# Building the operands of the last eight pairs a second time instead of storing and reloading them, and splitting the output weights every fourth product

## The chip, the cores and the metric

The kernel runs on one core of one Trainium2 chip. The metric is the device time of one execution in microseconds (us), as a median of several runs.

## The reference

One decoder block for a sequence of 2048 tokens with 1024 channels, all in float32:

```
h      = rms_norm(x, g_norm) * (1 + scale) + shift      # shift, scale, gate from silu(c) @ w_mod
proj   = h @ w_in                                       # (2048 x 1024) @ (1024 x 8192)
x_rnn, z_rnn, q, k, v, z_attn, g_r, g_a = split(proj)   # eight parts of 1024 columns
y_rnn  = (rg_lru(conv(x_rnn)) * silu(z_rnn)) @ w_out_rnn
y_attn = (dilated_attention(rope(q), rope(k), v) * silu(z_attn)) @ w_out_attn
merged = sigmoid(g_r + bg_r) * y_rnn + sigmoid(g_a + bg_a) * y_attn
out    = rms_norm(x + gate * (merged @ w_o), g_final)
```

The change is in how the weights of the large product `h @ w_in` (all parts but v) and of `w_out_rnn` and `w_out_attn` are prepared for the tensor engine.

## The kernel before

**Precision.** A float32 number is used as a high part and a low part. `split_s` (line 208) makes both of a weight block: ScalarE copies it to the rounded type (`hi_act`, line 158), and GpSimd (POOL) subtracts that copy from the block (`lo_pool`, line 164). `mm3` (line 152) then does three matmuls: high by high, high by low, low by high.

**Pairs and products.** The 7168 columns of `w_in` other than v are taken 256 at a time, in 28 pairs of 128-column blocks. `pair_order` (line 1143) gives their order: eight recurrent pairs `("r", m)`, with gate pairs and "plain" query and key pairs between them, and then the last six, two rotated pairs (the 32 columns of each head that get rotary angles) with two plain ones behind each. The last six run in a stage of their own with its own buffers, and pairs 20 and 21 are the last two of the stage before it. A pair is multiplied by Strassen's scheme in seven products instead of eight (`strassen`, line 349), each of four `mm3` of 128x512, twelve matmuls. Their left operands are the blocks a11, a21, a22, a12 or sums of them; the right ones (B11, T2, T3, T1, B21, T4, B22) come from h. The products add up in PSUM tiles X, Z, W, V and Y. ScalarE copies X out after the first product (`u1`, line 385), VectorE adds Z and W to it (`u2`, `u3`), and the fifth product is added into X again, so it must wait for `u1`. The last product of a pair (into V) is held until after the first of the next pair.

**Two halves.** The tokens are done in two halves, `f` = 0 and 1 (1024 tokens each), each with the values stage (`values_half`) and then 28 x 7 = 196 products. In the first half each left operand is made from raw weights, by `operand_events` (line 263): for pair `x` it yields steps with a due time in products, counted from four products (`LEAD`) ahead of the pair's first. Raw loads of a11, a21, a22 and a12 (SyncE's queue, SP, line 253) come at -6, -5, -4 and -1, two sums and a split at 0, and so on to the last split at 6; three sums beside them run on VectorE (lines 284, 285, 293 and 298 in all). Two splits later, ScalarE's queue stores the finished operand (512 KB, high and low) to `sD` in HBM (lines 276 and 279). In the second half `load_next` (line 313) loads all 196 operands back from `sD` through SP, seven ahead.

Operands live in a ring of seven tiles `S0` to `S6`, raw blocks in a ring of five, `R0` to `R4`. `pump` runs due steps after each product; `late` and `after_prod` hold other steps by product number. The order of instructions on each engine is written out by hand (`manual_schedule`), so each engine's queue is in the order in which these steps are emitted.

**Other work at these places.** `output_weights` (line 422) splits the 32 half blocks of `w_out_rnn` and `w_out_attn` during the second half: load (a raw tile), a raw copy to `wR` for the second matrix, split into the tiles `s1` and `s2`, and store to `wD`, one block every five products. The sums of `operand_events` use tiles `s1` and `s2` too. At the end of the first half `next_norm` and `next_even` load x for the next half (line 512), square its rows on ScalarE (line 1242) and build right operands from it; at the end of the second, `residual_gate` sums w_mod columns on VectorE. When `load_next` is past the operands it loads the first output weights (`load_wd`) for the next stage, attention; the last four operands bring with them a load of `yaT` each (`load_yd`, line 346), four blocks that are split (`yh`, `yl`) before the first matmul of that stage.

Of the kernel before, what the change touches and what calls it, by code (L numbers as in the profile page):

```python
# [20 lines left out]
P = 128  # L21
# [6 lines left out]
KH = KT // 2  # L28
# [5 lines left out]

FILL = (2.85, 2.75)
MORE = 0.8
NEG = 1e30

TABLES = 24
# [14 lines left out]
def constants():  # L54
# [10 lines left out]
    old, prev, diag = q4, (d <= 0) + q4, np.where(d >= 0, 1 + q4, 0)  # L65
    add = np.array([NEG, 0.0, -math.log(2.0)])
    cst[:, K_M23 : K_M23 + 512] = add[np.concatenate([old, old, prev, diag], axis=1)]
# [22 lines left out]
def decoder_block(ctx, tc, x, c, positions, g_norm, w_mod, b_mod, w_in, b_gate, conv_w, conv_b,  # L90
# [10 lines left out]
    def scratch(name, shape):  # L101
        return nc.dram_tensor(name, shape, F32, kind="Internal").ap()
# [8 lines left out]
    yaT = scratch("yaT", [D, S])  # L111
# [4 lines left out]

    tabD = scratch("tabD", [2, 2, P, HALF])

    sD = scratch("sD", [28 * 7, P, 2, KH, P])

    wD = scratch("wD", [2, KT, 2, P, 2, KH, P])
    wR = scratch("wR", [KT, 2, P, KH, P])
# [34 lines left out]
    def hi_act(o, i):  # L157
        nc.scalar.activation(o, i, AF.Copy)  # L158
# [4 lines left out]
    def lo_pool(o, i, h):  # L163
        nc.gpsimd.tensor_tensor(o, i, h.bitcast(F32), ALU.subtract)  # L164
# [26 lines left out]
    def s_tile(shape):  # L191
        i = ring["S"] % NS
        ring["S"] += 1
        return T(pS if i < 4 else wS, shape, F32R, f"S{i}")
# [13 lines left out]
    def split_s(src):  # L208
        t = s_tile([P, 2, KH, P])
        hi_act(t[:, 0], src)  # L210
        lo_pool(t[:, 1], src, t[:, 0])
        return t
# [3 lines left out]
    n_prod, late, after_prod = [0], {}, {}  # L216
# [18 lines left out]
    kept = []  # L235
# [25 lines left out]
    LEAD = 4  # L261

    def operand_events(x, pieces):

        load, v = block_loads(pieces), {}
        tt = nc.vector.tensor_tensor

        def raw(name, i, half):
            v[name] = load(i, half)

        def split(i, name):
            first[7 * x + i] = t = split_s(v[name])
            kept.append((7 * x + i, t))
            if len(kept) > 2:
                k, t2 = kept.pop(0)
                nc.scalar.dma_start(sD[k], t2[:].bitcast(F32))
            while 7 * x + i == 28 * 7 - 1 and kept:
                k, t2 = kept.pop(0)
                nc.scalar.dma_start(sD[k], t2[:].bitcast(F32))

        def sums():
            for name in ("s1", "s2"):
                v[name] = T(wq, [P, KH, P], F32, name, bufs=1)[:]
            tt(v["s1"], v["a21"], v["a22"], ALU.add)
            tt(v["s2"], v["s1"], v["a11"], ALU.subtract)  # L285

        yield -6, lambda: raw("a11", 0, 0)
        yield -5, lambda: raw("a21", 1, 0)
        yield -4, lambda: raw("a22", 1, 1)
        yield -1, lambda: raw("a12", 0, 1)  # L290
        yield 0, sums
        yield 0, lambda: split(0, "a11")
        yield 1, lambda: tt(v["a21"], v["a11"], v["a21"], ALU.subtract)
        yield 1, lambda: split(1, "s2")
        yield 2, lambda: split(2, "a21")
        yield 3, lambda: split(3, "s1")
        yield 4, lambda: split(4, "a12")
        yield 5, lambda: tt(v["s2"], v["a12"], v["s2"], ALU.subtract)
        yield 5, lambda: split(5, "a22")
        yield 6, lambda: split(6, "s2")  # L300

    first, events = {}, []
# [10 lines left out]
    def load_next():  # L313
        n = n_loaded[0]
        n_loaded[0] += 1
        if n < 28 * 7:
            t = s_tile([P, 2, KH, P])
            nc.sync.dma_start(t[:].bitcast(F32), sD[n])
            loaded.append((n, t))
            if n >= 28 * 7 - KH:  # L320
                load_yd(yaT, 0, n - 28 * 7 + KH)
        else:
            k = n - 28 * 7
            if k < 3:
                load_wd(0, 0, k) if k < 2 else load_wd(0, 1, 0)
            if k == 1:

                t = T(hp, [P, KH, CH], F32, "T", bufs=14)
                nc.sync.dma_start(t[:], yaT[KH * P :, :CH].rearrange("(k p) j -> p k j", p=P))
                for i in range(KH):  # L330
                    Y0[True, 0, KH + i] = t[:, i, :]
# [10 lines left out]
    def load_yd(ys, n, k):  # L342
        x = n_y[0]
        n_y[0] += 1
        t = T(pR, [P, CH], F32, f"R{x % 4}")
        nc.sync.dma_start(t[:], ys[k * P : (k + 1) * P, n * CH : (n + 1) * CH])
        Y0[ys is yaT, n, k] = t

    def strassen(f, key, done):

        up = pu[0]
        x = pair_id[key]
        if f and x == 0:
            for _ in range(NS):
                load_next()
        n_op = iter(range(7 * x, 7 * x + 7))

        def take():
            if f:
                return (f, *loaded.pop(0))  # L360
            i = next(n_op)
            return f, i, first.pop(i)

        def prod(ps, b, first, last, op=None):
            f, i, s = op or take()
            bh, bl = B[b]
            for k in range(KH):
                mm3(ps[:], s[:, 0, k, :], s[:, 1, k, :], bh[:, k, :], bl[:, k, :],
                    first=first and k == 0, last=last and k == KH - 1, skip_group_check=True)
            n_prod[0] += 1  # L370
            if f:
                used.add(i)
                while n_loaded[0] - NS in used:
                    load_next()
            run_late(n_prod[0])

        X = T(pj, [P, CH], F32, "X", bufs=2)
        prod(X, "B11", True, False)
        last_product()
        Z = T(pj, [P, CH], F32, "Z")  # L380
        prod(Z, "T2", True, True)
        u1 = T(up, [P, CH], F32, "u1", bufs=1)
        u2 = T(up, [P, CH], F32, "u2", bufs=2)
        with tc.high_priority():
            nc.scalar.activation(u1[:], X[:], AF.Copy)  # L385
            nc.vector.tensor_tensor(u2[:], Z[:], u1[:], ALU.add)
        W = T(pj, [P, CH], F32, "W")
        prod(W, "T3", True, True)
        u3 = T(up, [P, CH], F32, "u3", bufs=1)
        with tc.high_priority():  # L390
            nc.vector.tensor_tensor(u3[:], W[:], u2[:], ALU.add)
        V = T(pj, [P, CH], F32, "V")
        prod(V, "T1", True, False)
        done(1, 1, V, u3)
        prod(X, "B21", False, True)
        done(0, 0, X, None)
        Y = T(pj, [P, CH], F32, "Y")
        prod(Y, "T4", True, True)
        done(1, 0, Y, u3)
        op = take()  # L400

        def last():
            prod(V, "B22", False, True, op)
            done(0, 1, V, u2)
        behind.append(last)
# [16 lines left out]
    def output_weights():  # L422

        parts = [(i, w, m, half) for i, w in enumerate((w_out_rnn, w_out_attn)) for m in range(KT) for half in range(2)]
        for x, (i, w, m, half) in enumerate(parts):
            v = {}

            def load(v=v, w=w, m=m, half=half):
                v["raw"] = raw_tile([P, KH, P])
                rows = slice(half * KH * P, (half + 1) * KH * P)  # L430
                nc.sync.dma_start(v["raw"][:], w[0, rows, m * P : (m + 1) * P].rearrange("(k p) m -> p k m", p=P))

            def split(v=v):
                v["h"] = T(wq, [P, KH, P], F32R, "s1", bufs=1)
                v["l"] = T(wq, [P, KH, P], F32R, "s2", bufs=1)
                hi_act(v["h"][:], v["raw"][:])
                lo_pool(v["l"][:], v["raw"][:], v["h"][:])

            def store(v=v, i=i, m=m, half=half):
                for l, n in enumerate("hl"):  # L440
                    nc.scalar.dma_start(wD[i, m, half, :, l], v[n][:].bitcast(F32))

            def store_raw(v=v, m=m, half=half):
                nc.scalar.dma_start(wR[m, half], v["raw"][:])

            for d, fn in ((1, load), (3, store_raw), (4, split), (6, store)) if i else ((1, load), (4, split), (6, store)):
                after_prod.setdefault(n_prod[0] + 5 * x + d, []).append(fn)

    def total(dst, ps, u, perm=lambda ap: ap):

# [659 lines left out]
    for t in range(6):  # L1110
        pieces = []
        i0 = t * P
        while i0 < (t + 1) * P:
            hd, i = divmod(i0, 96)
            n = min(96 - i, (t + 1) * P - i0)
# [150 lines left out]

    for x, (key, pieces) in enumerate(pair_order()):
        pair_id[key] = x
        events += [(7 * x + d - LEAD, len(events) + i, fn) for i, (d, fn) in enumerate(operand_events(x, pieces))]
    events.sort(key=lambda e: e[:2])  # L1270
    for f in range(2):
        if f:
# [19 lines left out]
        n = 0  # L1292
# [504 lines left out]
    with tc.manual_schedule():  # L1797
# [8 lines left out]
        for s in range(first, max(end, len(units) + LAG + 1)):  # L1806
            rate = FILL[0] if s < NU * H + LAG else FILL[1]
            owed += rate + (MORE if 0 <= s <= NU else 0.0)

# [251 lines left out]
    with tc.manual_schedule():  # L2061
# [10 lines left out]
        for p in range(NP):  # L2072
            for d, fn, args in left_events(p):
                x = 7 * p + d - 4
# [54 lines left out]
```

## Time and profile before

| | |
|---|---|
| time, median of 3 runs | 2211.68 us (2210.36 to 2215.5) |
| the profiled execution, its own time | 2214.49 us |
| its span, first to last instruction | 2212.7 us |
| TensorE busy | 2162.3 us, 98% |
| VectorE, ScalarE, POOL busy | 1439.8, 1287.9 and 1003.4 us |
| moved by DMA | 573.41 MB, mean 259 GB/s |
| stores to `sD`, loads from it | 196 each, 512 KB each |

The products of the first half end at about 720 us, those of the second at about 1372 us. In the rows of the profile L12 is line 12 of the kernel; PE is TensorE's matmul, PEld its weight load, DVE is VectorE, ACT ScalarE, and SPq and ACTq are the instructions with which SyncE and ScalarE issue DMAs. In a row of the order of time, the start and the length in us come first, and in brackets the idle time ahead of it with what ended it. In a row of a group, busy time and the mean length in ns stand behind the first bar, idle time behind the second.

### The profile page before, as it was taken

How to read it: one execution, taken by the hardware profiler on the slowest of the kernel's cores; microseconds unless marked ns; L12 is line 12 of the kernel's file. 1: busy time of each engine (PE TensorE's matmuls, PEld its weight loads, DVE VectorE, ACT ScalarE, POOL GpSimd, SP SyncE). 2: the span in 40 equal slices, each digit the busy share in tenths (PEclk: the TensorE clock that was granted, in tenths of full speed). 3: DMA queues.
4: the chain of work that ended last, by engine and by line, in shares of the span. 5: the costliest groups of instructions: out<-in, count | busy, mean ns of one | idle time of the engine just before them, and what ended most of it. 6: DMA issues, size and time to landing. Idle time of an engine off the chain costs nothing.

```text
span 2212.7 us, 34220 instructions
## 1 busy us (share of the span) xinstructions
PE 2162.3 (98%) x11326; PEld 1831.0 (83%) x11326; DVE 1439.8 (65%) x2534; ACT 1287.9 (58%) x2570; POOL 1003.4 (45%) x756
## 2 busy tenths in 40 slices
PE   7999999999999999999999999999999999999998
PEld 4998888888777998888888887878888988887886
DVE  5928888878646724554445353566777777688787
ACT  5737777668543626556556411677888887444333
POOL 2448677767656423223222111455666664300443
PEclk9999999999999999999999999999999999999999
DMA  8367887887999467888988998978897876899542
GB/s 277 112 204 258 285 298 262 299 277 261 324 288 287 155 197 264 297 278 276 317 292 299 339 343 258 284 244 244 275 270 222 251 238 227 295 313 297 181 168 108
DMA packets 412277, 573.41 MB, mean 259 GB/s; under 512 B 72422, under 2 KB 270274, under 8 KB 411076
## 3 DMA queue, kind: packets, MB, share of 16 engines
q1 hardware_dynamic: 369892, 442.82, 63.3%
q10 hardware_dynamic: 42016, 128.36, 15.1%
q8 instruction: 90, 1.47, 0.3%
q14 instruction: 87, 0.71, 0.1%
q0 software_dynamic: 192, 0.05, 0.0%
HBM read 352.99 MB, written 218.11 MB: 258 GB/s over the span
## 4 chain that ended last, share of the span: by engine, by line
PE 54%; DMA 4%; issue 3%; ACT 3%; DVE 2%; POOL 2%; SPq 1%; ACTq 0%; POOLq 0%; DVEq 0%
PE X L150 10%; PE pj L150 10%; PE V L150 9%; PE W L150 5%; PE Z L150 5%; PE Y L150 4%; PE sc L150 3%; PE o L150 3%; PE pg L150 1%; PE pT L1506 1%; DMA vraw<-vN 1%; PE pT L1519 1%; ACT pp L1422 1%; ACT pp L1486 1%; DMA R<-in_w_in_dram 1%
## 5 line engine op out<-in xcount | busy, mean ns | idle before, releaser
L150 PE MATMUL pj<-yh,S 128*128 128x512 f32 x896 | 325.3, 404 | 5.5 <-DVE st L1421 1.9
L150 PE MATMUL X<-T,S 128*128 128x512 f32 x1344 | 326.0, 391 | 4.8 <-ACT u L385 4.3
L164 POOL TENSOR_TENSOR S<-R,S 128x512 fp32r<-128x512 f32 x168 | 252.6, 1512 | 171.4 <-ACT S L158 75.1
L150 PE MATMUL V<-T,S 128*128 128x512 f32 x1344 | 324.4, 390 | 1.9 <-DVE t L455 1.6
L150 PEld LDWEIGHTS X<-T,S 128*128 128x128 f32 x1344 | 252.6, 189 | 60.1 <-ACT u L385 5.6
L150 PEld LDWEIGHTS V<-T,S 128*128 128x128 f32 x1344 | 251.8, 188 | 56.1 <-DVE t L455 2.0
L150 PEld LDWEIGHTS pj<-yh,S 128*128 128x128 f32 x896 | 168.3, 188 | 37.6 <-ACT yh L158 3.3
L164 POOL TENSOR_TENSOR S<-s,S 128x512 fp32r<-128x512 f32 x92 | 140.6, 1528 | 118.0 <-ACT S L158 72.1
L150 PE MATMUL pj<-yl,S 128*128 128x512 f32 x448 | 176.2, 393 | 2.5 <-DVE yl L167 1.5
L1422 ACT ACTIVATE pp<-pp,st 128x256 f32<-128x256 f32 (+3 forms) x256 | 133.4, 523 | 60.4 <-DVE st L1421 59.9
L150 PE MATMUL Z<-T,S 128*128 128x512 f32 x672 | 162.0, 390 | 0.0
L150 PE MATMUL Y<-T,S 128*128 128x512 f32 x672 | 161.8, 390 | 0.0
L150 PE MATMUL W<-T,S 128*128 128x512 f32 x672 | 161.6, 389 | 0.0
L150 PEld LDWEIGHTS W<-T,S 128*128 128x128 f32 x672 | 126.0, 188 | 27.0 <-issue 0.9
L167 DVE TENSOR_TENSOR ptl<-pT,pth 128x384 fp32r<-128x384 f32 (+1 forms) x160 | 97.9, 629 | 77.2 <-ACT pth L158 75.0
L150 PEld LDWEIGHTS Y<-T,S 128*128 128x128 f32 x672 | 125.9, 188 | 26.1
L150 PEld LDWEIGHTS Z<-T,S 128*128 128x128 f32 x672 | 125.8, 188 | 26.1
L164 POOL TENSOR_TENSOR s<-R,s 128x512 fp32r<-128x512 f32 x32 | 46.7, 1459 | 204.3 <-ACT s L158 184.4
L913 DVE SCALAR_TENSOR_TENSOR xc<-xr,par,xc 128x512 f32<-128x512 f32 x96 | 98.7, 1028 | 46.2 <-ACT xc L907 44.0
L158 ACT ACTIVATE S<-R 128x512 fp32r<-128x512 f32 x168 | 101.4, 621 | 41.5 <-DMA R<-in_w_in_dram 14.6
L1486 ACT ACTIVATE pp<-pp,M 128x256 f32<-128x256 f32 (+3 forms) x256 | 118.0, 522 | 9.6 <-DVE M L1609 9.6
L158 ACT ACTIVATE S<-s 128x512 fp32r<-128x512 f32 x100 | 62.3, 623 | 97.2 <-DVE s L285 74.7
(423 smaller groups left out, 4938.7 us busy)
## 6 DMA issues: line engine op xcount, KB each, us to landing
sD<-S ACTq DMA_DIRECT2D x196, 512.0 KB, 4.3
S<-sD SPq DMA_DIRECT2D x196, 512.0 KB, 5.1
S<-wD SPq DMA_DIRECT2D x82, 512.0 KB, 5.2
R<-in_w_in_dram SPq DMA_DIRECT2D x136, 256.0 KB, 4.4
wD<-s ACTq DMA_DIRECT2D x64, 256.0 KB, 5.6
T<-in_w_mod_dram SPq DMA_DIRECT2D x8, 1024.0 KB, 11.6
vN<-ev SPq DMA_DIRECT2D x64, 128.0 KB, 2.7
zaT<-ev SPq DMA_DIRECT2D x32, 256.0 KB, 4.6
```

The lines of the kernel that those rows point to most:

```text
L150: nc.tensor.matmul(o, lhsT=l, rhs=r, start=st, stop=sp, **kw)
L158: nc.scalar.activation(o, i, AF.Copy)
L164: nc.gpsimd.tensor_tensor(o, i, h.bitcast(F32), ALU.subtract)
L167: return nc.vector.tensor_tensor(o, i, h.bitcast(F32), ALU.subtract).ins
L913: nc.vector.scalar_tensor_tensor(xc, xr[:, i : i + CH], cw(i), xc, ALU.mult, ALU.add)
L1422: nc.scalar.activation(pdst, pdst, AF.Exp, bias=m_, scale=-1.0, accum_out=l_)
L1486: nc.scalar.activation(pp, pp, AF.Copy, scale=w)
L1506: nc.tensor.transpose(pt[:, c0 + j * P : c0 + (j + 1) * P], pp[i][:, k * P : (k + 1) * P], ident)
L1519: nc.tensor.transpose(pt[:, c * P : (c + 1) * P], pp[:, half * P : (half + 1) * P], ident)
```

## The change

Of the 28 pairs, the operands of the first 20 (`REBUILT`) are stored and loaded back as before. For pairs 20 to 27 the first half stores nothing, and in the second half the same steps run again, 28 x 7 products later: raw loads, sums and splits. `load_next` then does nothing for these operands, and `strassen` takes them from the splits. The loads of `yaT`, which went with the last four operands, move behind the second and third load of output weights (two each). The blocks of the output weights come every four products, and each is stored one product after its split instead of two.

```diff
+REBUILT = 20
...
-    sD = scratch("sD", [28 * 7, P, 2, KH, P])
+    sD = scratch("sD", [REBUILT * 7, P, 2, KH, P])
...
         def split(i, name):
             first[7 * x + i] = t = split_s(v[name])
+            if x >= REBUILT:
+                return
             kept.append((7 * x + i, t))
             if len(kept) > 2:
                 k, t2 = kept.pop(0)
                 nc.scalar.dma_start(sD[k], t2[:].bitcast(F32))
-            while 7 * x + i == 28 * 7 - 1 and kept:
+            while 7 * x + i == REBUILT * 7 - 1 and kept:
...
     def load_next():
         n = n_loaded[0]
         n_loaded[0] += 1
-        if n < 28 * 7:
+        if n < REBUILT * 7:
             t = s_tile([P, 2, KH, P])
             nc.sync.dma_start(t[:].bitcast(F32), sD[n])
             loaded.append((n, t))
-            if n >= 28 * 7 - KH:
-                load_yd(yaT, 0, n - 28 * 7 + KH)
-        else:
+        elif n >= 28 * 7:
             k = n - 28 * 7
+            for y in range(2 * k - 2, 2 * k) if k in (1, 2) else ():
+                load_yd(yaT, 0, y)
...
         def take():
-            if f:
+            if f and x < REBUILT:
                 return (f, *loaded.pop(0))
...
-            for d, fn in ((1, load), (3, store_raw), (4, split), (6, store)) if i else ((1, load), (4, split), (6, store)):
-                after_prod.setdefault(n_prod[0] + 5 * x + d, []).append(fn)
+            for d, fn in ((1, load), (3, store_raw), (4, split), (5, store)) if i else ((1, load), (4, split), (5, store)):
+                after_prod.setdefault(n_prod[0] + 4 * x + d, []).append(fn)
...
     for x, (key, pieces) in enumerate(pair_order()):
         pair_id[key] = x
-        events += [(7 * x + d - LEAD, len(events) + i, fn) for i, (d, fn) in enumerate(operand_events(x, pieces))]
+        for f in range(1 + (x >= REBUILT)):
+            events += [(7 * (28 * f + x) + d - LEAD, len(events) + i, fn) for i, (d, fn) in enumerate(operand_events(x, pieces))]
```

## The prediction

> **What bounds the kernel now.** I read the profile page first, then the table of stretches, then TensorE's waits in the stretch that showed a loss, then the order of time around each loss, and last the DMA queues of the stretches that the change touches.
>
> ```profile
> span 2212.7 us, 34220 instructions
> PE 2162.3 (98%) x11326; PEld 1831.0 (83%) x11326; DVE 1439.8 (65%) x2534; ACT 1287.9 (58%) x2570; POOL 1003.4 (45%) x756
> 550.00:600.00 50.00, 48.88 (x214) 39.79 (x213) 33.47 (x39) 32.43 (x51) 31.40 (x22) 1.00 0.93 305
> 600.00:650.00 50.00, 46.89 (x198) 37.78 (x197) 25.76 (x42) 23.57 (x39) 28.81 (x19) 0.97 0.92 298
> 650.00:700.00 50.00, 48.03 (x214) 39.04 (x213) 31.06 (x39) 15.19 (x26) 33.58 (x22) 1.00 0.95 302
> 1250.00:1300.00 50.00, 50.00 (x223) 41.39 (x222) 23.50 (x33) 9.52 (x16) 8.14 (x6) 1.00 1.01 351
> 1300.00:1350.00 50.00, 50.00 (x216) 39.49 (x215) 21.22 (x33) 2.99 (x5) 5.48 (x4) 1.00 0.85 284
> ```
>
> The page says that TensorE is the bound: 2162.3 of 2212.7 us, 50 us idle. The five rows below it are stretches; their columns are busy us (and instructions) of PE, PEld, DVE, ACT and POOL, granted clock, DMA share and GB/s. The change touches the end of the products of the first half (about 545 to 720 us) and of the second (about 1215 to 1372 us). In the first, TensorE runs 198 to 214 matmuls in 50 us at a DMA share of 0.92 to 0.95; in the second it is never idle, although DMA is just as full. So there is something to win in the first half, and in the second there is only something to lose. What TensorE waits for from 540 to 725 us, and where in time:
>
> ```profile
> PE X L150 <- ACT u L385: 3.9, 2, 3.0
> PE pg L532 <- DVE hf L549: 2.2, 1, 2.2
> PE V L150 <- DVE t L455: 1.6, 1, 1.6
> PE X L150 <- POOL S L164: 0.4, 1, 0.4
> PE V L150 <- DVE ev L455: 0.2, 1, 0.2
> ...
> 575.62 2.88 PE L150 MATMUL V<-T,S 128*128 128x512 f32 x12
> 579.38 3.02 PE L150 MATMUL X<-T,S 128*128 128x512 f32 x12 [0.88 <-ACT u L385]
> 585.36 3.03 PE L150 MATMUL V<-T,S 128*128 128x512 f32 x12 [0.24 <-DVE ev L455]
> 621.42 4.61 PE L150 MATMUL X<-T,S 128*128 128x512 f32 x12 [2.99 <-ACT u L385]
> 628.62 3.31 PE L150 MATMUL X<-T,S 128*128 128x512 f32 x12
> 671.63 3.03 PE L150 MATMUL V<-T,S 128*128 128x512 f32 x12 [1.62 <-DVE t L455]
> 718.97 0.66 PE L532 MATMUL pg<-cs,x 128*128 128x128 f32 x4 [2.22 <-DVE hf L549]
> ```
>
> An undisturbed product (twelve matmuls) shows 2.88 us and starts 2.72 us after the one before it (its end overlaps the next). I put the losses into four terms.
> A, at 579 and 585: 0.88 + 0.24 idle, and two products longer by 0.14 and 0.15: 1.4 us.
> B, at 621: 2.99 idle, then a product of 4.61 (1.73 too long) and one of 3.31 (0.43 too long): 5.2 us.
> C, at 671: 1.62 + 0.15, and the 0.4 behind POOL: 2.2 us.
> D, at 719: 2.2 us.
> Together 11.0 us. They are all that can be won.
>
> TensorE's clock matters in B. The row of 4.61 us stands right behind the only gap of about 3 us, and the stretch 600 to 650 is the only one of the five with a granted clock under 1.00 (0.97). So a gap of 3 us costs 2.2 us more than it lasts. [...]
>
> **What holds up B and C.** The rows are ScalarE's around B, VectorE's ahead of C, and the queues and issues from 600 to 720 us (median us from issue to landing last).
>
> ```profile
> 611.71 1.06 ACT L1242 ACTIVATE hf<-x 128x1024 bf16<-128x1024 f32 x1 [8.28 <-DMA x<-in_x_dram]
> 616.76 0.34 ACTq L276 DMA_DIRECT2D sD<-S  x1
> 617.14 1.06 ACT L1242 ACTIVATE hf<-x 128x1024 bf16<-128x1024 f32 x1 [3.24 <-DMA R<-in_w_in_dram]
> 620.79 0.57 ACT L385 ACTIVATE u<-X 128x512 f32<-128x512 f32 x1
> 667.95 0.69 DVE L284 TENSOR_TENSOR s<-R,R 128x512 f32<-128x512 f32 x1 [7.13 <-DMA R<-in_w_in_dram]
> ...
> q1 hardware_dynamic: 36985, 16.03, 50.7%
> q10 hardware_dynamic: 5313, 19.32, 41.6%
> L512 SPq DMA_DIRECT2D x<-in_x_dram x2: 742/1270/1797, 602.0 to 604.2; - x2
> x<-in_x_dram SPq DMA_DIRECT2D x2, 1024.0 KB, 10.7
> R<-in_w_in_dram SPq DMA_DIRECT2D x24, 64.0 KB, 4.6
> ```
>
> ScalarE executes in order. The squares of x stand ahead of the copy `u1` out of X, and TensorE may add the fifth product into X only after that copy. ScalarE sat 8.28 us for x, then 3.24 us in which its queue held a store to `sD` (issued at 616.76), and `u1` came at 620.79. X's next product was due at 621.42 - 2.99 = 618.4, so `u1`, done at 621.4, was 3.0 us late. At C it is VectorE that waits 7.13 us for raw weights, and the sums out of V queue behind that. Of the DMA time in this stretch, 41.6 points of about 92 are queue q10, ScalarE's: the stores to `sD`.
>
> **The change part by part.** First half, stores. Pairs 20 to 27 have 56 operands.
>
> ```profile
> L276 ACTq DMA_DIRECT2D sD<-S x53: 326/327/895, 548.3 to 699.5; - x53
> S<-sD SPq DMA_DIRECT2D x196, 512.0 KB, 5.1
> R<-in_w_in_dram SPq DMA_DIRECT2D x136, 256.0 KB, 4.4
> ```
>
> 56 stores of 512 KB (29.4 MB) go, and 56 x 0.33 = 18 us of ScalarE's queue with them, spread over 548 to 701 us (the row counts 53 of them by one line; the last go from another). The DMA share there falls from 0.92 to about 0.51. A: 53 stores in 151 us are 4.6 in the 13 us ahead of 579, 1.5 us of ScalarE's queue, and `u` was 0.88 late: A goes, 1.4. B: `u1` must be 3.0 us earlier. The 3.24 us I put down to the store issued at 616.76 rather than to the raw load that the row names, and x itself should land earlier: B goes, bar 0.2: 5.0. C hangs on landings of raw weights, and SP's own order of issue is part of their delay, which stays: I count half, 1.1. D hangs on weights and x loads of the next stage, whose stores have ended by then: 0.5, from between 0 and 2.2. Sum for the first half: 8.0 us.
>
> Second half, work. The 56 loads of `sD` (29.4 MB) go, 32 loads of raw weights (8.4 MB) come; the program moves 573.4 - 50.3 = 523 MB. Splitting comes to an engine that is nearly free there:
>
> ```profile
> L158 ACT ACTIVATE S<-R 128x512 fp32r<-128x512 f32 x168 | 101.4, 621 | 41.5 <-DMA R<-in_w_in_dram 14.6
> L164 POOL TENSOR_TENSOR S<-R,S 128x512 fp32r<-128x512 f32 x168 | 252.6, 1512 | 171.4 <-ACT S L158 75.1
> L284 DVE TENSOR_TENSOR s<-R,R 128x512 f32<-128x512 f32 x28 | 33.0, 1177 | 28.5 <-DMA R<-in_w_in_dram 24.5 <-DMA qT<-t 4.0
> ```
>
> 56 x 0.62 = 35 us on ScalarE, 56 x 1.51 = 85 us on POOL, and 8 pairs x 4 sums of at most 1.18 = 38 us on VectorE, over some 157 us. On top of the rows for 1250 to 1350 that is about 35% busy on ScalarE, 68% on POOL, 69% on VectorE: none becomes the bound. Per product of 2.72 us POOL needs 1.51. What covers all this is the lead of four products, 10.9 us, between a split and its product. What can break it is order: a late raw load now holds up VectorE, ScalarE and POOL in the second half as it does at C, with the evictions, the rotary steps and `u1` queued behind. The squares of x, which made B, are not there. The nearest rows give from 0 to C's whole 2.2 per such event. I take the half of C that I left in the first half: 1.1 us lost.
>
> Second half, order. Loads of `yaT` move five and three products later, behind the last raw slots, on SP ahead of `wD`.
>
> ```profile
> 1357.51 0.44 SPq L346 DMA_DIRECT2D R<-yaT  x1
> 1365.02 0.54 SPq L340 DMA_DIRECT2D S<-wD  x1
> 1367.39 2.18 ACT L158 ACTIVATE yh<-R 128x512 fp32r<-128x512 f32 x4
> 1373.13 0.47 PE L150 MATMUL pj<-yh,S 128*128 128x512 f32 x1 [0.83 <-issue]
> R<-yaT SPq DMA_DIRECT2D x4, 256.0 KB, 4.5
> ```
>
> The last two now leave with the load at 1365.0 and land about 1370.4; their splits end near 1372.5 and TensorE uses the third of them 1.4 us after 1373.1. It fits with 2 us to spare at this landing; the queue is emptier by then. Between 0 and 2 us, I take 0.4, as a landing of 7 us would cost it all and 4.5 nothing.
>
> Output weights every fourth product instead of fifth, stores one product after the split instead of two. The same 32 parts end at product 129 instead of 161. The store waits on ScalarE for POOL's subtraction (1.5 us); behind it queues `u1`, due three products (8.2 us) after its source. From 800 to 1350 us TensorE shows no idle, so 0; if the cover fails, 1.5 us at a part.
>
> Sum: 8.0 - 1.1 - 0.4 = 6.5 us won. The profiled execution took 2214.5 us (1.8 beside its span of 2212.7), which is 2.8 above the median of the runs, 2211.7. So 2208.0 by the profile's own time, and 2205.2 as a median.
>
> **The rivals.** Differences of 0.2% (4.4 us) are about what a measurement of this kernel can tell from none.
>
> *The stores were not the cause.* x lands late because SP issues it late (the second at 604.2) and it is 1 MB, and ScalarE's squares sit ahead of `u1` anyway. For it: both x loads took 10.7 us in the median. Against it: 41.6 points of DMA time go. Then only A and a little of B are won, 2.5, less 1.5 lost: 2210.7, no change. Chance 0.2.
>
> *Slower: late raw weights in the second half.* VectorE, SP and ScalarE there are in a chain that before was only in the first half. It decides where a raw load lands more than 10.9 us (four products) after its event, with SP's queue ahead of it. The rows show small pieces (64 KB, 24 issues) in 4.6 us, but VectorE's wait of 7.13 shows that it happened once with DMA full. Were it to happen at each of the six pairs of the rotary stage, 6 x 2.2, and one gap passed 3 us (2.2 more), 15.4 would be lost against 8.0 won: 2219.1. [...] Chance 0.13.
>
> *All of it goes.* C and D vanish with the traffic, and the second half loses nothing: 2211.7 - 11.0 = 2200.7. Chance 0.17. That the change does not do what it says I exclude: the early return drops the stores, and the ring of slots keeps its order.
>
> **How the numbers follow.** Forecast 0.5. The range takes the case of all of it and something beyond (the 0.83 us at 1373, an earlier eviction), 2199, and at the other end the first rival with the whole unknown of order lost, 2213.5; outside lie the slower rival and a little more, 0.18. Faster by over 0.2% (under 2207.3): 0.17 and nearly all of the forecast: 0.65. Slower (over 2216.1): 0.13. Same: 0.22.
>
> **What would show it.** Right: no `sD` stores after about 548 us; about 523 MB moved; a DMA share near 0.5 from 560 to 700; no TensorE gap at 621 and no granted clock below 1.00 there; 220 matmuls in 50 us; POOL two thirds busy at the end of the second half with TensorE still without idle. Wrong: TensorE waits for ScalarE's `u` or VectorE's `t` in the second half, or x still landing after 10 us.

## The result, and the profile after

The change makes the kernel faster: 2204.51 us in the median (2202.16 to 2212.85, 11 runs) against 2214.59 for the kernel before on the same chips (2210.14 to 2220.12, 11 runs), the three of the table above among them. The ratio is 0.9956 with a 95% interval of 0.9943 to 0.9969, or 9.8 us (6.9 to 12.6). The profiled execution took 2208.98 us.

First the profile page after, and the same stretches as before the change (busy us and instructions of PE, PEld, DVE, ACT and POOL, granted clock, DMA share, GB/s):

```profile
span 2207.1 us, 34359 instructions
PE 2164.0 (98%) x11326; PEld 1832.7 (83%) x11326; DVE 1483.4 (67%) x2566; ACT 1318.3 (60%) x2626; POOL 1092.1 (49%) x812
DMA packets 434166, 523.08 MB, mean 237 GB/s; under 512 B 104550, under 2 KB 306498, under 8 KB 432964
sD<-S ACTq DMA_DIRECT2D x140, 512.0 KB, 4.1
S<-sD SPq DMA_DIRECT2D x140, 512.0 KB, 5.3
...
500.00:550.00 50.00, 48.39 (x213) 39.69 (x212) 38.61 (x39) 39.00 (x62) 36.66 (x24) 1.00 0.68 239
550.00:600.00 50.00, 48.81 (x214) 39.72 (x214) 36.02 (x41) 33.64 (x52) 32.39 (x22) 1.00 0.57 150
600.00:650.00 50.00, 50.00 (x222) 41.44 (x221) 28.49 (x45) 26.41 (x44) 31.94 (x22) 1.00 0.66 158
650.00:700.00 50.00, 50.00 (x229) 41.37 (x228) 32.84 (x44) 16.00 (x28) 34.24 (x25) 1.00 0.43 111
1250.00:1300.00 50.00, 50.00 (x222) 41.40 (x222) 39.19 (x45) 15.19 (x28) 34.55 (x22) 1.00 0.67 171
1300.00:1350.00 50.00, 50.00 (x216) 39.50 (x215) 33.52 (x43) 14.26 (x25) 34.55 (x23) 1.00 0.56 138
```

140 operands (20 pairs of seven) are stored and loaded back, for 196 before. From 600 to 700 us TensorE is now never idle and never slowed. DMA is a little over half full in both places (shares of 0.43 to 0.67). In the second half POOL went from 8.14 to 34.55 busy us of 50, VectorE from 23.50 to 39.19, and TensorE still has no idle. But from 500 to 600 us it loses 2.8 us, for 1.1 before. Its waits from 540 to 725 us, and the order of time of TensorE and ScalarE where they fall:

```profile
PE X L151 <- ACT u L388: 2.6, 2, 1.6
PE V L151 <- DVE ev L458: 0.2, 1, 0.2
...
539.94 3.02 PE L151 MATMUL X<-T,S 128*128 128x512 f32 x12 [1.61 <-ACT u L388]
580.68 3.02 PE L151 MATMUL X<-T,S 128*128 128x512 f32 x12 [0.95 <-ACT u L388]
586.66 3.02 PE L151 MATMUL V<-T,S 128*128 128x512 f32 x12 [0.24 <-DVE ev L458]
...
537.69 1.56 ACTq L282 DMA_DIRECT2D sD<-S  x2
539.29 0.60 ACT L388 ACTIVATE u<-X 128x512 f32<-128x512 f32 x1 [5.78 <-POOL S L165]
```

B, C and D are gone. A, at 580, is as it was, and there is a new gap at 540: ScalarE stood 5.78 us ahead of `u1`, behind the flush of the last stores (line 282).

The products start at the same time in both (142.4 us). Those of the second half start at 803.98 us instead of 812.20, and the first matmul behind them at 1364.90 instead of 1373.13. So 8.2 us are won by then, all before the second half's products, and those cost nothing: they take 560.92 us for 560.93. This one execution then gives back 2.6 us in the stages behind, to end 5.6 us earlier. That last stretch took between 838.9 and 844.5 us in the profiles of all twelve kernels of this document, without regard to the change.

DMA of both places, 560 to 700 us after, and 1230 to 1360 us before and then after:

```profile
q1 hardware_dynamic: 49727, 19.77, 56.5%
R<-in_w_in_dram SPq DMA_DIRECT2D x42, 64.0 KB, 2.8
x<-in_x_dram SPq DMA_DIRECT2D x2, 1024.0 KB, 9.2
L515 SPq DMA_DIRECT2D x<-in_x_dram x2: 432/1214/1995, 594.6 to 596.6; - x2
...
DMA packets 22602, 41.00 MB, mean 315 GB/s; under 512 B 2097, under 2 KB 12337, under 8 KB 22594
1230.00:1360.00 130.00, 130.00 (x569) 105.73 (x568) 55.00 (x79) 24.55 (x38) 17.21 (x13) 1.00 0.94 315
DMA packets 44187, 21.58 MB, mean 166 GB/s; under 512 B 30833, under 2 KB 40609, under 8 KB 44178
R<-in_w_in_dram SPq DMA_DIRECT2D x32, 64.0 KB, 2.7
1230.00:1360.00 130.00, 130.00 (x569) 105.76 (x568) 86.19 (x103) 42.73 (x75) 81.05 (x55) 1.00 0.64 166
```

Queue q10 has nothing left to do at the end of the first half. Small raw loads land in 2.8 us instead of 4.6. x still takes 9.2 us to land (10.7 before), but SyncE gets to issue it at 594.6 instead of 602.0.

### The profile page after: what moved, and what is told of

The parts are those of the page before. It is cut to its first block, busy times and chain, and to the rows that moved or that the text cites. A ratio compares the mean times of both kernels' runs of the same rounds, so it can differ in the third digit from the quotient of the medians.

```text
span 2207.1 us, 34359 instructions
## 1 busy us (share of the span) xinstructions
PE 2164.0 (98%) x11326; PEld 1832.7 (83%) x11326; DVE 1483.4 (67%) x2566; ACT 1318.3 (60%) x2626; POOL 1092.1 (49%) x812
## 4 chain that ended last, share of the span: by engine, by line
PE 57%; DMA 6%; issue 3%; POOL 3%; DVE 2%; ACT 1%; SPq 1%; POOLq 0%; ACTq 0%; DVEq 0%
PE X L151 12%; PE V L151 11%; PE pj L151 9%; PE W L151 6%; PE Z L151 6%; PE Y L151 5%; PE sc L151 4%; PE o L151 3%; PE pg L151 1%; PE pT L1510 1%; PE pT L1523 1%; DMA S<-wD 1%; POOL kq L165 1%; POOL q L1387 1%; DMA mrT<-fg 1%
## 5 line engine op out<-in xcount | busy, mean ns | idle before, releaser
L165 POOL TENSOR_TENSOR S<-R,S 128x512 fp32r<-128x512 f32 x200 | 312.4, 1570 | 180.9 <-ACT S L159 85.1
L165 POOL TENSOR_TENSOR S<-s,S 128x512 fp32r<-128x512 f32 x116 | 172.8, 1490 | 144.1 <-ACT S L159 107.9
L159 ACT ACTIVATE S<-s 128x512 fp32r<-128x512 f32 x124 | 77.4, 624 | 131.6 <-DVE s L288 101.1
L159 ACT ACTIVATE S<-R 128x512 fp32r<-128x512 f32 x200 | 120.8, 621 | 55.5 <-PE Z L151 9.3
## 6 DMA issues: line engine op xcount, KB each, us to landing
T<-in_w_mod_dram SPq DMA_DIRECT2D x8, 1024.0 KB, 11.7
```

## The experiments

My theory was that the stores' traffic in the first half is the whole cause. The rivals were that ScalarE's queue is held by issues and waits, that the second half has a part in it, and that a part of the change has a price of its own. Every ratio is to the kernel before, timed beside it; the numbers of the profiles are from one execution each.

**1. Only the first half.** The kernel before, without the stores of pairs 20 to 27.

```diff
+            if x >= 20:
+                return
             kept.append((7 * x + i, t))
...
-            nc.sync.dma_start(t[:].bitcast(F32), sD[n])
+            nc.sync.dma_start(t[:].bitcast(F32), sD[n if n < 140 else n - 56])
```

> The kernel before without the stores of pairs 20 to 27 in the first half; in the second half, their loads fetch operands 56 places earlier instead (same size, wrong values), so the second half does the same work as before. If the whole gain comes from the first half, this is 8 to 10 us faster than before, as much as the change. If the rebuilding in the second half gained or cost something, it differs from the change's 9.8 us by that, beyond 3 us. The new gap near 540 us (1.6 us, behind the flush of the last stores) should be here too.

Ratio 0.995 (0.9935 to 0.9965), 11.1 us faster. That is the change's 0.9956 within the intervals: the first half holds the whole gain. The gap near 540 us is here too, as expected (1.16 us).

**2. The same stores with an eighth of the bytes.**

```diff
                 k, t2 = kept.pop(0)
-                nc.scalar.dma_start(sD[k], t2[:].bitcast(F32))
+                if k < 140:
+                    nc.scalar.dma_start(sD[k], t2[:].bitcast(F32))
+                else:
+                    nc.scalar.dma_start(sD[k, :, 0, 0], t2[:, 0, 0, :].bitcast(F32))
...
```

The flush of the last stores is edited alike, and the loads as in the first run.

> As the kernel before, but each store of pairs 20 to 27 writes one 128x128 block of eight (64 KB instead of 512 KB): ScalarE issues and waits as often, an eighth of the bytes move. The loads of the second half fetch operands 56 places earlier (wrong values). If the stores' traffic was the cause: 7 to 10 us faster than before. If ScalarE's queue, held by issues and by waits for POOL, was the cause: under 3 us faster.

Ratio 0.9947 (0.9929 to 0.9965), 11.7 us. All the issues and their waits are still on ScalarE, and everything is won. TensorE's waits from 530 to 725 us, and ScalarE's queue from 560 to 700, before and then in this run:

```profile
PE X L150 <- ACT u L391: 0.5, 1, 0.5
PE V L150 <- DVE ev L461: 0.2, 1, 0.2
...
q10 hardware_dynamic: 6912, 25.17, 46.4%
q10 hardware_dynamic: 7200, 3.28, 8.4%
sD<-S ACTq DMA_DIRECT2D x50, 64.0 KB, 2.6
```

So it was the bytes, 46 points of DMA time down to 8, and not ScalarE's queue as such. A store of an eighth also lands sooner (2.6 us for 4.4) and gives its tile in the ring back sooner, which no run separates from its traffic. In the profile before, though, waits for a store to land come to only 1.0 us on ScalarE from 545 to 725 us, and to none on VectorE, POOL or TensorE.

**3. The same traffic from SyncE.**

```diff
-                nc.scalar.dma_start(sD[k], t2[:].bitcast(F32))
+                (nc.scalar if k < 140 else nc.sync).dma_start(sD[k], t2[:].bitcast(F32))
...
```

> As the kernel before, but the stores of pairs 20 to 27 are issued by SyncE instead of ScalarE: all the traffic, nothing in ScalarE's queue. If ScalarE's queue was the cause: 5 us faster or more. If traffic was the cause: within 2 us of before, or slower, as SyncE's raw loads now queue behind stores that wait for POOL.

Ratio 1.0007 (0.9996 to 1.0017): nothing won. The losses are not the old ones, though. TensorE's gaps from 595 to 700 us:

```profile
627.22 4.63 PE L150 MATMUL X<-T,S 128*128 128x512 f32 x10 [4.13 <-POOL S L164]
691.51 4.63 PE L150 MATMUL X<-T,S 128*128 128x512 f32 x10 [4.28 <-POOL S L164]
```

The wait for `u` at 621 is gone, and TensorE waits instead for operands that POOL has not finished. Ahead of both gaps VectorE stood 5.04 and 5.98 us for the stores of rotated q and k (`qT`, `kT`), which SyncE issues too, and the sums and the subtractions on POOL came behind that. Here the stores to `sD` stand in the same queue, so this run alone would not tell traffic from order; the second one does.

**4. All stores kept, the second half rebuilt.** The changed kernel, whose first half stores all operands again.

```diff
...
-            if x >= REBUILT:
+            if not first_pass:
                 return
...
```

(`first_pass` holds while the steps run in the first half; the scratch `sD` and the flush at its end go back to 28 pairs)

> The changed kernel, but the first half stores all operands as before (and nobody loads the last 56). The second half is that of the change. If rebuilding in the second half costs nothing, within 2 us of before. If late raw loads stall TensorE there, slower by 2 us or more, with waits for u or t between 1215 and 1375 us. If the second half is where the change gains, faster by 5 or more.

Ratio 0.9999 (0.9987 to 1.0011). TensorE's waits from 530 to 725 us are on the same steps as before and 8.5 us in all, for 8.3; from 800 to 1376 us there is the last of these rows alone, which is in all kernels:

```profile
PE X L151 <- ACT u L388: 4.0, 2, 3.6
PE V L151 <- DVE t L458: 2.1, 1, 2.1
PE pg L535 <- DVE hf L552: 1.5, 1, 1.5
PE X L151 <- POOL S L165: 0.7, 1, 0.7
PE V L151 <- DVE ev L458: 0.2, 1, 0.2
...
PE pj L151 <- issue: 0.8, 1, 0.8
```

The second half neither wins nor loses. With the first run this settles where the gain is.

**5. A later flush.**

```diff
             if x >= REBUILT:
+                if kept:
+                    k, t2 = kept.pop(0)
+                    nc.scalar.dma_start(sD[k], t2[:].bitcast(F32))
                 return
...
-            while 7 * x + i == REBUILT * 7 - 1 and kept:
-                k, t2 = kept.pop(0)
-                nc.scalar.dma_start(sD[k], t2[:].bitcast(F32))
```

> The changed kernel, but the last three stores of pair 19 are no longer flushed at once behind its last split: each goes out with one of the next three splits, as stores did before. If the flush, which waits on ScalarE for POOL's last subtraction, made the new gap near 540 us, that gap (1.6 us idle and 0.1 behind it) is gone and the kernel is 1 to 2 us faster than the change, some 11 us faster than before. If the gap has another cause, it stays, at some 10 us faster than before.

Ratio 0.9949 (0.9936 to 0.9961), 11.3 us. The gap at 540 is gone from the trace, so the flush made it. Against the change's 9.8 us the 1.5 us lie within both intervals, so the time does not show it. A is still there:

```profile
578.98 3.03 PE L151 MATMUL X<-T,S 128*128 128x512 f32 x12 [1.26 <-ACT u L388]
```

**6. `u1` ahead of the steps of the second product**, on top of the late flush.

```diff
-        prod(Z, "T2", True, True)
         u1 = T(up, [P, CH], F32, "u1", bufs=1)
...
             nc.scalar.activation(u1[:], X[:], AF.Copy)
+        prod(Z, "T2", True, True)
+        with tc.high_priority():
```

> As the late flush, and the copy u1 of X stands on ScalarE ahead of the steps that follow the second product, not behind them. If the gaps at about 580 us in both kernels come from ScalarE's own backlog (table loads and splits ahead of u1), and not from stores or traffic, the waits of TensorE for u between 530 and 600 us are gone: about 1 us faster than the late flush alone, and 12 us faster than before. If not, no faster than the late flush, or slower, where ScalarE now waits for X with work behind it.

Ratio 0.9962 (0.995 to 0.9975), no better than the late flush. The waits for `u` are gone, as expected, but another stands in their place:

```profile
588.43 4.37 PE L151 MATMUL V<-T,S 128*128 128x512 f32 x12 [2.49 <-DVE ev L459]
```

There ScalarE works without idle from 568.6 to 582.7 us, and VectorE, which waits 3.77 us for one of its results, without idle from 578.7 us to past the sum that TensorE waits for (at 587.6). So another step is late when `u1` is put first.

**7. x two products earlier, in the kernel before.**

```diff
-        later(3, lambda: xs.extend(load_x(xp, 2, "x", 2)))
+        later(1, lambda: xs.extend(load_x(xp, 2, "x", 2)))
```

> The kernel before, with the loads of x at the end of the first half issued two products (5.4 us) earlier; all stores stay. [...] If ScalarE is held there by its stores and not by x, within 2 us of before.

Ratio 0.9999 (0.999 to 1.0007): nothing. The time is the one expected if x were not the cause, but the trace does not show that cause. SyncE's issue of x, then ScalarE and TensorE:

```profile
L512 SPq DMA_DIRECT2D x<-in_x_dram x2: 333/495/657, 596.4 to 598.1; - x2
614.08 0.63 ACT L158 ACTIVATE S<-R 128x512 fp32r<-128x512 f32 x1 [6.92 <-DMA R<-in_w_in_dram]
617.07 5.46 PE L150 MATMUL V<-T,S 128*128 128x512 f32 x12 [5.50 <-ACT S L158]
688.47 2.57 PE L150 MATMUL X<-T,S 128*128 128x512 f32 x10 [2.79 <-POOL S L164]
```

x was issued 5.6 us earlier and ScalarE waited 3.82 us for it instead of 8.28, so the gap at 621 is gone; but the raw weights issued behind it came late, and a gap of 5.50 us at 617 took its place. Here, with all stores kept and x taking 12.1 us to land (10.7 before), an earlier issue moved the loss and did not remove it.

**8. Output weights every fourth product, alone, in the kernel before.**

```diff
-                after_prod.setdefault(n_prod[0] + 5 * x + d, []).append(fn)
+                after_prod.setdefault(n_prod[0] + 4 * x + d, []).append(fn)
```

(and the store one product after the split)

> The kernel before with one part of the change alone: output weights every fourth product, stored one product after the split. If that costs nothing, within 2 us of before, with no wait of TensorE from 800 to 1375 us beyond the 0.8 at its end. If stores waiting on ScalarE hold u1, slower by 1.5 us or more with waits for u there.

Ratio 0.9997 (0.9984 to 1.001), and no wait of TensorE from 800 to 1376 us but the 0.8 at its end. This part costs nothing. Up to the end of the first half this kernel is the kernel before, so its profile also shows how much the losses vary from one execution to the next: D is 0.71 us in it for 2.22, and A's first gap 0.53 for 0.88.

**9 and 10. How many pairs.** The late flush with other values of `REBUILT`.

```diff
-REBUILT = 20
+REBUILT = 22      # 25 in the second of the two
```

> The late flush with REBUILT at 22 instead of 20: only the last stage's six pairs are built twice, and pairs 20 and 21 are stored and loaded again. Their stores fall ahead of about 590 us, where the gap at 579 us does not come from traffic. If the gain hangs on DMA being free behind 590 us, as with the late flush: 9 to 11 us faster than before. If every pair's stores count alike, three quarters of the gain: 7 to 8 us.

> The late flush with REBUILT at 25: the stores stop at about 645 us. If each loss goes with the traffic at its own place, the loss at 621 us (5 us) stays and those at 671 and 719 us go: 3 to 5 us faster than before. If stores ahead of 645 us do not matter, as much as with 22.

With 22 the ratio is 0.9947 (0.9934 to 0.996), 11.7 us; with 25 it is 0.997 (0.9959 to 0.9982), 6.6 us (4.0 to 9.1), where 3 to 5 was expected. Stretches with 22, then with 25, and the gaps of TensorE with 25:

```profile
550.00:600.00 50.00, 49.57 (x218) 40.36 (x217) 33.87 (x40) 31.99 (x50) 33.57 (x23) 1.00 0.93 295
600.00:650.00 50.00, 50.00 (x222) 41.41 (x221) 27.71 (x42) 26.45 (x44) 34.23 (x24) 1.00 0.64 147
...
600.00:650.00 50.00, 46.68 (x198) 37.80 (x197) 24.69 (x39) 22.30 (x37) 28.12 (x19) 0.97 0.90 282
650.00:700.00 50.00, 50.00 (x230) 41.37 (x229) 34.59 (x45) 17.59 (x30) 37.06 (x27) 1.00 0.59 148
...
574.94 3.01 PE L151 MATMUL X<-T,S 128*128 128x512 f32 x12 [0.18 <-ACT u L388]
617.04 4.62 PE L151 MATMUL X<-T,S 128*128 128x512 f32 x12 [3.17 <-ACT u L388]
```

The losses go where the traffic goes. With 25, DMA is still 0.90 full from 600 to 650 us and the gap of B is there, while behind 650, where the stores have stopped, TensorE is full. With 22, stores up to 583 us do no harm, at a DMA share of 0.93. That version has 0.4 us of TensorE's waits left from 530 to 725 us and by the ratio is as good as any here; it is not shown to beat the change.

The profiles of all twelve kernels can be set side by side by two lengths. From the first product of the first half to the first of the second, the five kernels that keep all stores at full size take 668.0 to 672.6 us (669.8 before). Those without full stores from 590 us on take 657.9 to 664.9 (661.5 for the change, 657.9 for small stores), and the one whose stores stop at 645 us takes 663.2. From there to the first matmul behind the products of the second half it is 560.9 us in eleven of them and 561.3 with the late flush, whether the operands are loaded or rebuilt.

## Why the prediction was right

It forecast 6.5 us won (2205.2, between 2199.0 and 2213.5), and 2204.51 was measured. That the two times lie within 0.7 us is luck: the forecast starts from 2211.68, and the kernel before took 2214.59 in the runs beside the change. The gain is the fair comparison: 9.8 us by the ratio, with an interval whose lower end of 6.9 is just above the forecast of 6.5. By its steps:

- *The place.* Right: everything to win lay in the first half. The first and the fourth run show it from both sides.
- *B and the clock.* Right in size, 5.2 us gone whole, with no granted clock under 1.00 from 600 to 650. The working was off. I put it on ScalarE's blocked store and on x landing faster. x lands little faster (9.2 us for 10.7), but SyncE issues it 7.4 us earlier, and ScalarE starts its squares at 604.38 us without a wait, for 611.71 after 8.28 us of waiting. The small stores of the second run, with all their issues on ScalarE, won as much. What holds SyncE up ahead of x is not settled: its waits for transfers to land, from 560 to 600 us, fall from 6.2 us to 0.7 in the change, but are 6.1 in the second run, where x goes out early as well. Nor does it take a gap as long as B's 2.99 us for a surcharge: behind 2.49 us in the sixth run and 2.87 us in the eighth, a product took about 1.5 us more than the undisturbed 2.88 (4.37 and 4.35).
- *C and D.* Too small: I counted 1.1 of 2.2 and 0.5 of 2.2, and both went. What I took for SyncE's own order at C went with the traffic as well: the small raw loads land in 2.8 us, and VectorE's wait of 7.13 us for them is gone. Ahead of D, ScalarE stood 3.64 and 2.71 us for raw weights of the next stage. The prediction took their loads to be free of the stores; but SyncE issued most of them only from 710 us on, against 690 after the change, so it seems that they inherited the lateness. A wait of TensorE of 0.9 us for VectorE between 725 and 800 us is new.
- *A.* Wrong. It was to go with the stores' issue time, and stayed: 0.95 and 0.24 after, 1.26 with the late flush. In kernels whose stores go on there it was between 0.18 (`REBUILT` at 25) and 0.88 (before), in those without 0.94 to 1.26. So stores do not make it. The term that failed is the 1.5 us of ScalarE's queue for the issues of 4.6 stores. From the start of ScalarE's backlog to `u1`, before and then after:

```profile
565.81 0.72 ACT L1180 ACTIVATE ev<-ev,par 128x512 f32<-128x512 f32 x1 [1.17 <-DVE ev L455]
578.75 0.58 ACT L385 ACTIVATE u<-X 128x512 f32<-128x512 f32 x1
...
567.10 0.73 ACT L1183 ACTIVATE ev<-ev,par 128x512 f32<-128x512 f32 x1 [1.17 <-DVE ev L458]
580.05 0.57 ACT L388 ACTIVATE u<-X 128x512 f32<-128x512 f32 x1
```

That is 12.94 us with five stores issued in it and 12.95 with none, and ScalarE has no idle in either: the issues cost it nothing there, and its own backlog makes `u1` late. Moving `u1` only moved the gap. Why the gap is 0.18 in one kernel and 1.26 in another stays open.

- *The flush.* Missed: it stands behind pair 19 now instead of the last pair, and ScalarE's wait there costs 1.6 us of TensorE. The term was not in the sum.
- *The second half's work and order.* I took 1.1 and 0.4 us off; both are 0. The rival "slower" needed raw loads that land later than 10.9 us after their event; the small ones land 2.7 us after their issue there, and TensorE has no wait. DMA time fell by less than the bytes there: 1230 to 1360 us moves 21.58 MB instead of 41.00, with 30833 packets under 512 B instead of 2097, and the DMA share falls only from 0.94 to 0.64. Even so it is far from full.
- *Output weights.* Right, 0.

C, D and the second half were sized 4.3 us too small a gain in all, A and the flush 3.1 too large. With that, 6.5 becomes 7.7, and 6.8 with the new wait of 0.9, against 8.2 between the marks in the profile. So 1.4 us are in no term here (0.4 is a wait for `u` at 255 us, which the profile before has and that after has not), and that the errors nearly cancel is luck. What the measured 9.8 has beyond 8.2 lies inside its interval. The rival that the stores were not the cause falls with the second run.

## What to carry to other kernels

Where a tight engine loses time while DMA is full, look for bytes to drop at that place before looking for a better order: here an earlier load won nothing, and an eighth of the bytes with the same issues won all. Recomputing a stored operand pays where the engines that make it are idle in the second use, and it need only reach as far as the stretch that is full. A flush at the end of a stored series waits at once for what it stores; let it lag as the others do (here that took a gap of 1.6 us out of the trace, too little for the time to show).

## What the runs showed of the hardware that was not expected

The surcharge behind a gap of TensorE is no plain function of its length in these runs. Products of twelve matmuls behind gaps of 0.88 to 1.75 us took 3.02 to 3.03 us, against 2.88 undisturbed. Behind 2.49 us (sixth run) one took 4.37, behind 2.87 us (eighth) 4.35, behind 3.17 us (`REBUILT` at 25) 4.62 and behind 5.50 us (seventh) 5.46. But ten matmuls behind a gap of 2.79 us (seventh) took 2.57 us, as behind one of 0.41 (eighth, 2.56), and ten behind 4.13 us (third) took 4.63. So one gap of 2.49 us was charged and one of 2.79 was not. What decides that, no run here shows.
